# Modulation coefficients by sets of 128 features instead of 256, in a hybrid convolution and recurrence layer on one core

## Chip, core and metric

The kernel runs on one core of one Trainium2 chip. The metric is the device time in microseconds; the kernel before takes 1643.37 us (median of three runs, 1643.29 to 1644.09).

## What is computed

The layer has 256 latent tokens `x`, 256 context tokens `ctx` and 2048 features, all in float32. Only its first stage matters here. Both token streams are normalised, scaled and shifted, each with its own vectors (from `c` for the latents, from `c_ctx` for the context), and the result `h` goes into a large input projection:

```
mod = silu(c) @ w_mod + b_mod                   # w_mod 2048 x 12288, six vectors of 2048
sh_m, sc_m, ... = split(mod, 6)
h  = rms_norm(x,   norm_pre_mix) * (1 + sc_m)  + sh_m
hc = rms_norm(ctx, norm_pre_mix) * (1 + scc_m) + shc_m    # the same with silu(c_ctx)
p  = h @ w_in ;  pc = hc @ w_in[:, :3072]
```

The 4096 columns of `w_mod` that give `sh_m` and `sc_m` are 33.6 MB. They are read while the first products of `h` with `w_in` are made, because a block of 128 features of `h` needs only its own 128 scales and shifts.

## The kernel before

**Tiles and queue.** Weights come in tiles of 128 x 1024 floats (512 KB), all issued on SP's DMA queue in the order of a list (`Stream`, lines 414 to 427). A tile lands in one of 5 buffers called `raw`, or, if the list says `paged`, in one of 30 general pages of the same size (`page`, line 191; the trace calls it `rawpage`). `fetch_to(FETCH)` issues tiles ahead until 13 are held, 5 in `raw` buffers and 8 in pages (`RAWS`, `FETCH`, line 92). A page that is wanted while all 30 are held waits for the release of another. In this stage the pages also hold the inputs (8, until they are turned), the turned inputs `xT` (8, two blocks of 128 features each), the blocks `h` (one page each), and some single ones.

**Sets.** Features are handled in 8 sets of 256, that is two row blocks of 128 (loop at line 664). For one set the weights are 8 tiles. Of the 2048 rows of `w_mod`, the first 1536 (`KP` = 12 blocks of 128) go over TensorE: 12 products of a 128 x 32 operand `s32` (silu of both vectors, 2 of 32 columns used) with 128 x 512 weights (scale and shift of 256 features), four at a time in four column strips of 32 of the array (line 675). The last 512 rows go over VectorE: two tiles `wmd`, transposed on the host, and for each 4 multiplications with running sum (`sums`, line 648). `wmd` tiles lie in `raw` buffers, the other six in pages.

**From sums to h.** `modulate` (line 602) copies the TensorE sums to a row (ScalarE, line 605), turns it by 4 transposes, adds up the four strips (VectorE, line 612), adds the VectorE part and the bias, and has scale `A` and shift `B` of two blocks (lines 616, 619). Then, for each of the two blocks, ScalarE writes the rounded `h` and the full value back into `xT` (line 629, four instructions of 128 x 256), and VectorE writes the rest, their difference (line 632).

**Order on VectorE.** Calls of `issue_after` fix the order in which instructions are queued on an engine. `normed` (line 555, the multiplication of the next set's inputs by the reciprocal root mean square) is put behind the last line 632 of this set (line 703), and `sums` of the next set is put behind `normed` (line 665). So on VectorE one turn of the loop is: line 612, `A` and `B`, the two line 632, `normed`, the 8 sums of the next set, and line 612 again.

**Work between.** Tiles of `w_in` are split into a rounded part and a rest (`whi` on ScalarE, line 123, `wlo` on VectorE, line 126). `values` multiplies each block of `h` with half of a tile `wi0` (12 matmuls of 512 columns a block), `forget` with a quarter of a tile `wf0` (6 matmuls a block). They are generators whose pieces are put between the steps of `modulate` (lines 686 to 707), so that TensorE has work while the other engines make the next `h`. `values_begun` (24 matmuls) does blocks 0 and 1 of a second tile right after the first set. While the first set is awaited, TensorE makes 20 idle products in the same form (lines 676 to 678) and some `warm` matmuls. All TensorE instructions of the stage are queued in program order (`pe`, line 180).

Of the kernel before, what the change touches and what calls it, by code (L numbers as in the profile page):

```python
# [8 lines left out]
F32 = mybir.dt.float32  # L9
F32R = mybir.dt.float32r  # L10
# [27 lines left out]
KP = 12  # L38
FETCH = 13

# [11 lines left out]
class Stream:  # L52
# [76 lines left out]
    def next(self, ahead=AHEAD):  # L129
        while len(self.ready) < ahead and self.done < len(self.items):  # L130
            self.prepare()
        while ahead > 1 and self.done < len(self.items) and self.items[self.done][1] is not None:
            self.prepare()
        return self.ready.popleft()


class Kernel:
# [227 lines left out]
    def run(self):  # L365
# [143 lines left out]
        def block(k):  # L509

            return xT[k // 2][:, k % 2 * 512:(k % 2 + 1) * 512]
# [36 lines left out]

        def normed(c, *behind):

            x = xT[c][:, :TW].rearrange("p (j t) -> p j t", j=2)
            with ExitStack() as after:
                for ins in behind:
                    after.enter_context(self.tc.issue_after(ins.ins))
                self.last3 = nc.vector.tensor_tensor(x, x, rrow.rearrange("p (o t) -> p o t", o=1).broadcast_to([P, 2, 512]), op=ALU.mult)

# [15 lines left out]

        fq = collections.deque()

        def forget():
# [25 lines left out]

        def modulate(c, ps, part):

            row = self.small(512, "row")
            self.last = nc.scalar.copy(out=row, in_=ps)
            yield
            pt = self.bank()
            for j in range(4):
                self.pe(nc.tensor.transpose, out=pt[:, j * P:(j + 1) * P], in_=row[:, j * P:(j + 1) * P], identity=v["ident"])

            cols = self.small(8, "cols")
            nc.vector.tensor_reduce(cols.rearrange("p (j i) -> p j i", i=2), pt.rearrange("p (j g f) -> p j f g", j=4, g=4)[:, :, 0:2, :],
                                    axis=mybir.AxisListType.X, op=ALU.add)
            ks = slice(2 * c, 2 * c + 2)
            for n, dst in enumerate((Av, Bv)):
                nc.vector.tensor_tensor(dst[:, :, ks], cols[:, 4 * n:4 * n + 4].rearrange("p (b i) -> p i b", i=2),
                                        part[:, 4 * n:4 * n + 4].rearrange("p (b i) -> p i b", i=2), op=ALU.add)
                if n == 0:
                    self.scaled = nc.vector.scalar_tensor_tensor(dst[:, :, ks], dst[:, :, ks], 1.0,
                                                                 v["g_pm"][:, ks].rearrange("p (o k) -> p o k", o=1).broadcast_to([P, 2, 2]), op0=ALU.add, op1=ALU.mult)  # L620
            yield
            for k in range(2 * c, 2 * c + 2):
                hp.append(self.page(F32R, f"h{k}"))
                hi, lo = (hp[k].rearrange("p (i s t) -> p s i t", i=2, s=2)[:, n] for n in range(2))
                x = block(k).rearrange("p (i t) -> p i t", i=2)
                with self.tc.issue_after(self.his[-1].ins):
                    for o in (hi, x):
                        for i in range(2):
                            last = nc.scalar.activation(out=o[:, 1 - i], in_=x[:, 1 - i], func=AF.Identity, scale=Av[:, i, k:k + 1], bias=Bv[:, i, k:k + 1])  # L629
                for i in range(2):  # L630
                    hparts[i].append(hp[k][:, (1 - i) * 512:(2 - i) * 512])
                self.last2 = last, nc.vector.tensor_tensor(lo, x, hi.bitcast(F32), op=ALU.subtract)
                yield

        def sums(c, *behind):

            part = self.cp.tile([P, 8], F32, name="part", tag="part", bufs=2)
            for u in range(2):
                st.fetch_to(FETCH)
                w = st.whole()  # L640
                for b in range(2):
                    s = w[:, b * 512:(b + 1) * 512]
                    for i in range(2):
                        o = s if i else self.small(512, "junk")
                        with ExitStack() as after:
                            for ins in behind:
                                after.enter_context(self.tc.issue_after(ins.ins))
                            nc.vector.scalar_tensor_tensor(o, s, 1.0, srow[:, i * 512:(i + 1) * 512], op0=ALU.mult, op1=ALU.mult,
                                                           accum_out=part[:, 4 * u + 2 * b + i:4 * u + 2 * b + i + 1])
            for n in range(2):  # L650
                p = part[:, 4 * n:4 * n + 4].rearrange("p (b i) -> p b i", i=2)
                o = (1 - n) * KT + 2 * c
                nc.vector.tensor_tensor(p, p, v["bmod"][:, o:o + 2].rearrange("p (b o) -> p b o", o=1).broadcast_to([P, 2, 2]), op=ALU.add)
# [10 lines left out]
        for c in range(8):  # L664
            part = sums(c, self.last3)
            ps = self.bank()
            for t in range(KP // 2):
                st.fetch_to(FETCH)
                w = st.whole()
                for k2 in range(2):  # L670
                    k = 2 * t + k2
                    g = 32 * (k % 4)
                    self.pe(nc.tensor.matmul, ps[g:g + 32, :], s32[:, 32 * k:32 * k + 32], w[:, k2 * 512:(k2 + 1) * 512], start=(k < 4), stop=(k >= KP - 4))
                if c == 0 and t < KP // 2 - 1:

                    if t == 0:
                        idle = self.bank()
                    for g in range(0, P, 32):
                        self.pe(nc.tensor.matmul, idle[g:g + 32, :], s32[:, :32], srow[:, :512], start=True, stop=True)
            st.fetch_to(FETCH)  # L680

            mod = modulate(c, ps, part)
            next(mod)
            copied = self.last
            if c:
                next(forget)
            else:
                self.warm(5)
            next(mod)
            if c:  # L690
                next(forget)
            else:
                self.warm(8)
            parts(vq, copied, lo=[self.scaled])
            next(mod)
            if c == 0:
                parts(fq, *self.last2)
                parts(vq2, *self.last2)
            next(mod)
            if c % 2 and c < 7:  # L700
                parts(fq, *self.last2)
            if c < 7:
                normed(c + 1, *self.last2)
            for _ in range(2 if c else 1):
                next(values)
            for _ in range(2):
                next(forget)
            if c == 0:
                vb = self.values_begun(hx, vq2.popleft())
        for _ in values:  # L710
# [760 lines left out]
    def conv(self, uhv, uvv):  # L1471
# [73 lines left out]
_IN = [("pack", (P, NPACK), F32), ("x", (T, D), F32), ("ctx", (T, D), F32), ("bgain", (4, TW), F32), ("gain", (4, TW), F32), ("masks", (P, 7 * P), I32),  # L1545
       ("wm0", (4 * KP, P, TW), F32), ("wmd", (16, P, TW), F32), ("crow", (2, TW), F32), ("wmt", (64, P, TW), F32), ("wm1", (64, P, TW), F32), ("wi0", (16, P, TW), F32), ("wf0", (4, P, TW), F32), ("wi1", (80, P, TW), F32),
       ("wi2", (80, P, TW), F32),        ("wpw", (16, P, TW), F32), ("who", (16, P, TW), F32), ("wo", (32, P, TW), F32), ("w1", (128, P, TW), F32), ("w2", (128, P, TW), F32)]
# [76 lines left out]
```

## Time and profile before

| | |
|---|---|
| median of three runs | 1643.37 us |
| the profiled execution's own time | 1644.45 us |
| span of its instructions | 1642.7 us |
| TensorE busy | 1627.8 us, 99% of the span |
| VectorE busy | 1163.1 us, 71% |
| ScalarE busy | 799.9 us, 49% |
| bytes moved by DMA | 374.47 MB, 228 GB/s in the mean |

Times in the rows count from the span's start. PE is TensorE's matmuls, PEld its weight loads, DVE is VectorE, ACT is ScalarE, SP issues the DMAs. A float32 matmul that is not in the rounded format appears as two instructions, so the 12 products of a set are 24 rows. A matmul's length contains its latency: the next one can start long before it ends, so that paces are read from start to start.

### The profile page before, as it was taken

To read this page: it belongs to the slowest core of one execution; us is meant where nothing else is said; L and a number is where in the kernel's file an instruction comes from. 1 tells how busy PE (TensorE), PEld (TensorE's weight loads), DVE (VectorE), ACT (ScalarE), POOL (GpSimd) and SP (SyncE) were. 2 spreads that over 40 slices of the span, in tenths; PEclk is the share of its full clock that TensorE was granted. 3 is DMA by queue.
4 is the path that set the end of the run, shared out by engine and by line. 5 is a ranking of instruction groups with operands and counts; after the bars stand their busy time and mean duration, and the time that the engine had idled before them with its cause. 6 is when DMAs were issued, how large, how long until landed. Compare 5 with 4: busy or idle time off the path is not lost.

```text
span 1642.7 us, 22019 instructions
## 1 busy us (share of the span) xinstructions
PE 1627.8 (99%) x8211; PEld 1359.2 (83%) x8211; DVE 1163.1 (71%) x1703; ACT 799.9 (49%) x1142; POOL 8.1 (0%) x18
## 2 busy tenths in 40 slices
PE   8999999999999999999999999999999999999998
PEld 6668888888988888888888888888888888888887
DVE  7777777778868889967887766456655665566555
ACT  6553444443554444653446665445544554346543
POOL 0000000000000000000000000000000000000000
PEclk9999999999999999999999999999999999999999
DMA  9998954444656556688887376677667667666553
GB/s 375 389 395 292 318 163 149 154 142 141 204 185 227 189 187 210 228 277 294 317 291 269 136 233 204 212 237 240 219 205 232 233 214 215 232 219 195 190 192 116
DMA packets 103771, 374.47 MB, mean 228 GB/s; under 512 B 11632, under 2 KB 12400, under 8 KB 103664
## 3 DMA queue, kind: packets, MB, share of 16 engines
q1 hardware_dynamic: 102096, 368.60, 66.4%
q0 software_dynamic: 1280, 4.21, 0.9%
q8 instruction: 64, 1.05, 0.3%
q14 instruction: 43, 0.35, 0.1%
q10 hardware_dynamic: 288, 0.26, 0.0%
HBM read 370.93 MB, written 2.10 MB: 227 GB/s over the span
## 4 chain that ended last, share of the span: by engine, by line
PE 93%; DVE 2%; DMA 2%; ACT 1%; issue 1%; SPq 0%; ACTq 0%; DVEq 0%
PE bank L185 62%; PE bank L252 18%; PE bank L254 9%; PE bank L1396 2%; DMA raw<-wpw 1%; DVE wlo L126 1%; DMA x<-ctx 1%; DMA rawpage<-wm 1%; ACT whi L123 0%; PE bank L1427 0%; PE bank L1438 0%; PE bank L1436 0%; DVE gacc L1236 0%; SPq L498 0%; PE bank L1419 0%
## 5 line engine op out<-in xcount | busy, mean ns | idle before, releaser
L126 DVE TENSOR_TENSOR wlo<-raw,whi 128x1024 fp32r<-128x1024 f32 x488 | 594.7, 1224 | 356.2 <-ACT whi L123 348.4
L123 ACT ACTIVATE whi<-raw 128x1024 fp32r<-128x1024 f32 x488 | 513.4, 1059 | 577.7 <-PE bank L185 322.9
L185 PE MATMUL bank<-whi,h 128*128 128x512 f32 x1264 | 396.6, 392 | 0.8 <-ACT h L629 0.5
L252 PE MATMUL bank<-h,whi 128*128 128x512 f32 x1280 | 322.4, 394 | 0.0
L185 PEld LDWEIGHTS bank<-whi,h 128*128 128x128 f32 x1264 | 237.3, 188 | 50.9 <-DVE h L1085 0.7
L252 PEld LDWEIGHTS bank<-h,whi 128*128 128x128 f32 x1280 | 230.7, 189 | 41.3
L185 PE MATMUL bank<-wlo,h 128*128 128x512 f32 x632 | 246.9, 391 | 0.7 <-DVE wlo L126 0.5
L185 PE MATMUL bank<-whi,hidh 128*128 128x512 f32 x503 | 195.3, 388 | 0.0
L185 PE MATMUL bank<-wlo,hidh 128*128 128x512 f32 x503 | 195.3, 388 | 0.0
L185 PE MATMUL bank<-whi,hidl 128*128 128x512 f32 x503 | 195.3, 388 | 0.0
L254 PEld LDWEIGHTS bank<-h,wlo 128*128 128x128 f32 x1280 | 174.6, 190 | 12.6
L254 PE MATMUL bank<-h,wlo 128*128 128x256 f32 x1280 | 178.5, 283 | 0.0
L185 PE MATMUL bank<-h,whi 128*128 128x512 f32 x512 | 164.7, 403 | 0.0
L185 PEld LDWEIGHTS bank<-wlo,h 128*128 128x128 f32 x632 | 118.8, 188 | 26.5 <-DVE wlo L126 2.4
L185 PEld LDWEIGHTS bank<-whi,hidh 128*128 128x128 f32 x503 | 94.5, 188 | 19.3
L185 PEld LDWEIGHTS bank<-whi,hidl 128*128 128x128 f32 x503 | 94.5, 188 | 19.2
L185 PEld LDWEIGHTS bank<-wlo,hidh 128*128 128x128 f32 x503 | 94.5, 188 | 19.2
L185 PEld LDWEIGHTS bank<-h,whi 128*128 128x128 f32 x512 | 92.1, 189 | 21.4 <-issue 5.9
L185 PE MATMUL bank<-h,wlo 128*128 128x512 f32 x256 | 100.2, 391 | 0.0
L1236 DVE SCALAR_TENSOR_TENSOR gacc<-raw,silu_c,gacc 128x1024 f32<-128x1024 f32 x60 | 76.8, 1279 | 0.0
L1249 DVE SCALAR_TENSOR_TENSOR raw<-raw,silu_row 128x1024 f32<-128x1024 f32 x64 | 76.5, 1220 | 0.0
L185 PEld LDWEIGHTS bank<-h,wlo 128*128 128x128 f32 x256 | 48.1, 188 | 10.5 <-DVE wlo L126 0.3
(246 smaller groups left out, 1363.0 us busy)
## 6 DMA issues: line engine op xcount, KB each, us to landing
raw<-w SPq DMA_DIRECT2D x256, 512.0 KB, 4.3
raw<-wi SPq DMA_DIRECT2D x172, 512.0 KB, 4.4
raw<-wmt SPq DMA_DIRECT2D x64, 512.0 KB, 4.3
raw<-wm SPq DMA_DIRECT2D x64, 512.0 KB, 4.5
rawpage<-wm SPq DMA_DIRECT2D x48, 512.0 KB, 8.8
raw<-wo SPq DMA_DIRECT2D x32, 512.0 KB, 4.7
raw<-wmd SPq DMA_DIRECT2D x16, 512.0 KB, 8.6
raw<-who SPq DMA_DIRECT2D x16, 512.0 KB, 5.1
```

Of the source, the lines that this page charges most:

```text
L123: kn.his.append(nc.scalar.activation(out=hi, in_=raw, func=AF.Copy))
L126: kn.los.append(nc.vector.tensor_tensor(lo, raw, hi.bitcast(F32), op=ALU.subtract))
L185: ins = fn(*args, **kw)
L252: nc.tensor.matmul(bank, w[0][:, cut(i)], x(k)[2], start=(k == 0), stop=False)
L254: nc.tensor.matmul(bank[:, T:], w[1][:, cut(i)], x(k)[0], start=False, stop=(k == nk - 1))
L1236: nc.vector.scalar_tensor_tensor(acc, raw, s, acc, op0=ALU.mult, op1=ALU.add)
L1249: nc.vector.scalar_tensor_tensor(raw, raw, 1.0, self.srow, op0=ALU.mult, op1=ALU.mult, accum_out=self.dot[:, 32 * j + b:32 * j + b + 1])
L1396: nc.tensor.matmul(ps[:, b * P:(b + 1) * P], w, r, start=True, stop=True)
```

## The change

- Sets have 128 features, one block; there are 16. A set's matmuls have 256 columns (scale and shift of 128 features).
- In the first two sets all 16 row blocks go over TensorE (16 products, 4 tiles `wms`, no VectorE sums). In the other 14 a set has one tile `wmd` (4 sums) and three tiles `wm0` (12 products). The tiles of `w_mod` are 64 as before.
- All of them, `wmd` too, lie in pages; `FETCH` is 16, so up to 11 pages and 5 `raw` buffers are held ahead.
- In set k TensorE's queue has the products of the set, 3 matmuls of `forget`, 2 transposes, 3 matmuls of `forget`, 12 of `values`; from set 2 on all of these 18 are with block k-1. Blocks 0 and 1 of the second tile (24 matmuls) come in set 1. The idle products are 12, of 256 columns.
- The row's copy is queued behind ScalarE's last write for the block before, the reduction of line 612 behind the set's sums. Bias and scale are folded into two instructions for `A` and `B`.

```diff
-FETCH = 13
+WHOLE = 2
+FETCH = 16
...
-        for c in range(8):
-            for u in range(2):
-                st.add_whole(a["wmd"][2 * c + u])
-            for t in range(KP // 2):
-                st.add_whole(a["wm0"][KP // 2 * c + t], paged=True)
-            st.add(a["wi0"][c])
-            if c == 0 or c % 2 and c < 7:
-                st.add(a["wf0"][(c + 1) // 2])
-            if c == 0:
+        for k in range(KT):
+            if k < WHOLE:
+                for t in range(KT // 4):
+                    st.add_whole(a["wms"][KT // 4 * k + t], paged=True)
+            else:
+                st.add_whole(a["wmd"][k - WHOLE], paged=True)
+                for t in range(KP // 4):
+                    st.add_whole(a["wm0"][KP // 4 * (k - WHOLE) + t], paged=True)
+            if k % 2 == 0:
+                st.add(a["wi0"][k // 2])
+            if k == 0 or k % 4 == 3 and k < KT - 1:
+                st.add(a["wf0"][(k + 1) // 4])
+            if k == 1:
                 st.add(a["wi0"][8])
...
+        def modulate(k, ps, part):
+            row = self.small(T, "row")
+            with ExitStack() as after:
+                for ins in self.last2[:1] if k else ():
+                    after.enter_context(self.tc.issue_after(ins.ins))
+                self.last = nc.scalar.copy(out=row, in_=ps)
+            yield
+            pt = self.bank()
+            for j in range(2):
+                self.pe(nc.tensor.transpose, out=pt[:, j * P:(j + 1) * P], in_=row[:, j * P:(j + 1) * P], identity=v["ident"])
+            cols = self.small(4, "cols")
+            with ExitStack() as after:
+                if part is not None:
+                    after.enter_context(self.tc.issue_after(self.last5.ins))
+                nc.vector.tensor_reduce(...)
+            a_, b_ = cols[:, 0:2], cols[:, 2:4]
+            if part is not None:
+                nc.vector.tensor_tensor(a_, a_, part[:, 0:2], op=ALU.add)
+            self.scaled = nc.vector.tensor_scalar(out=Av[:, :, k], in0=a_, scalar1=bias1[:, k:k + 1], scalar2=v["g_pm"][:, k:k + 1], op0=ALU.add, op1=ALU.mult)
+            if part is not None:
+                self.scaled = nc.vector.scalar_tensor_tensor(Bv[:, :, k], b_, v["bmod"][:, k:k + 1], part[:, 2:4], op0=ALU.add, op1=ALU.add)
...
+            x = block(k).rearrange("p (i t) -> p i t", i=2)
+            with self.tc.issue_after(self.his[-1].ins):
+                for o in (hi, x):
+                    for i in range(2):
+                        last = nc.scalar.activation(out=o[:, 1 - i], in_=x[:, 1 - i], func=AF.Identity, scale=Av[:, i, k:k + 1], bias=Bv[:, i, k:k + 1])
...
+            self.last2 = last, nc.vector.tensor_tensor(lo, x, hi.bitcast(F32), op=ALU.subtract)
+            yield
+        def sums(k, *behind):
+            if k < WHOLE:
+                return None
...
+            for n in range(2):
+                s = w[:, n * 512:(n + 1) * 512]
                 for i in range(2):
+                    o = s if i else self.small(512, "junk")
...
+                        self.last5 = nc.vector.scalar_tensor_tensor(o, s, 1.0, srow[:, i * 512:(i + 1) * 512], op0=ALU.mult, op1=ALU.mult,
+                                                                    accum_out=part[:, 2 * n + i:2 * n + i + 1])
...
+        for k in range(KT):
+            part = sums(k, self.last3)
+            ps = self.bank()[:, :T]
+            nk = KT if k < WHOLE else KP
+            for t in range(nk // 4):
                 st.fetch_to(FETCH)
                 w = st.whole()
+                for j in range(4):
+                    g, n = 32 * j, 4 * t + j
+                    self.pe(nc.tensor.matmul, ps[g:g + 32, :], s32[:, 32 * n:32 * n + 32], w[:, j * T:(j + 1) * T], start=(t == 0), stop=(t == nk // 4 - 1))
...
+            mod = modulate(k, ps, part)
             next(mod)
             copied = self.last
+            if k:
                 next(forget)
...
             next(mod)
+            if k:
                 next(forget)
...
+            if k % 2 == 0:
+                parts(vq, copied, lo=[self.scaled])
+            if k == 1:
+                parts(vq2, copied, lo=[self.scaled])
             next(mod)
+            if k == 0 or k % 4 == 3 and k < KT - 1:
                 parts(fq, *self.last2)
+            if k < KT - 1:
+                normed(k + 1, *self.last2)
+            if k == 1:
+                vb = self.values_begun(hx, vq2.popleft())
+            else:
                 next(values)
```

`normed(k)` now multiplies one block (128 x 512), and `parts` splits a tile: `whi` on ScalarE behind the instructions named, `wlo` on VectorE.

## Rows read from the trace of the kernel before

**Rows 1.** The page's first part: engine, busy us (share of the span), instructions.

```profile
PE 1627.8 (99%) x8211; PEld 1359.2 (83%) x8211; DVE 1163.1 (71%) x1703; ACT 799.9 (49%) x1142; POOL 8.1 (0%) x18
```

**Rows 2.** The chain of waits that ended last, from 0 to 260 us, in order of time: start, length, what ran or was awaited.

```profile
5.35 11.43 DMA x<-ctx
...
31.40 37.88 PE bank L185 x199
...
70.73 8.92 DMA rawpage<-wm
...
79.69 24.57 PE bank L185 x128
...
104.30 64.03 PE bank L185 x294
```

**Rows 3.** The stretches of 10 us: start:end, length, then busy us (instructions) of PE, PEld, DVE, ACT and POOL, TensorE's granted clock as a share of full speed, DMA share, GB/s.

```profile
10.00:20.00 10.00, 9.89 (x74) 9.65 (x73) 8.41 (x15) 7.59 (x16) 0.00 (x0) 1.00 1.03 416
...
50.00:60.00 10.00, 10.00 (x57) 6.15 (x56) 9.56 (x26) 3.99 (x7) 0.00 (x0) 1.00 0.99 373
...
90.00:100.00 10.00, 10.00 (x58) 6.70 (x51) 7.35 (x24) 6.54 (x11) 0.00 (x0) 1.00 1.02 407
...
120.00:130.00 10.00, 10.00 (x46) 8.28 (x45) 4.16 (x5) 7.08 (x13) 0.00 (x0) 1.00 0.74 247
```

**Rows 4.** PE's instructions in order of time, from the inputs' last step to the first product with `h`: start, length, line, operation, count.

```profile
20.50 0.65 PE L185 MATMUL bank<-pack,r 128*128 128x128 f32 x4
21.08 0.62 PE L185 MATMUL bank<-rawpage,s 128*32 128x512 f32 x2
...
27.58 0.60 PE L185 MATMUL bank<-rawpage,s 128*32 128x512 f32 x2
28.11 0.77 PE L185 MATMUL bank<-ones_r 128*128 128x128 f32 x5
28.92 0.66 PE L185 MATMUL bank<-pack,row 128*128 128x128 f32 x4
...
30.89 0.50 PE L185 MATMUL bank<-whi,h 128*128 128x512 f32 x1 [0.47 <-ACT h L629]
31.40 0.50 PE L185 MATMUL bank<-wlo,h 128*128 128x512 f32 x1
```

**Rows 5.** PE's instructions in order of time around one set's products (the fourth set).

```profile
64.77 0.39 PE L185 MATMUL bank<-h,wlo 128*128 128x512 f32 x1
65.09 2.78 PE L185 MATMUL bank<-rawpage,s 128*32 128x512 f32 x24
67.80 0.73 PE L185 MATMUL bank<-h,whi 128*128 128x512 f32 x2
68.37 0.40 PE L185 MATMUL bank<-h,wlo 128*128 128x512 f32 x1
68.61 0.66 PE L185 MATMUL bank<-pack,row 128*128 128x128 f32 x4
69.02 0.71 PE L185 MATMUL bank<-h,whi 128*128 128x512 f32 x2
69.57 0.40 PE L185 MATMUL bank<-h,wlo 128*128 128x512 f32 x1
```

**Rows 6.** All engines in order of time in the middle of the second set's products; the count of a row takes in instructions that the window cuts off.

```profile
41.55 1.50 PE L185 MATMUL bank<-rawpage,s 128*32 128x512 f32 x12
...
42.01 0.13 PEld L185 LDWEIGHTS bank<-rawpage,s 128*32 128x32 f32 x4 [0.30 <-issue]
```

**Rows 7.** DVE's instructions in order of time, one turn of the loop (third set).

```profile
58.29 0.19 DVE L612 TENSOR_REDUCE cols<-bank 128x8 f32<-128x32 f32 x1
...
58.79 1.23 DVE L126 TENSOR_TENSOR wlo<-raw,whi 128x1024 fp32r<-128x1024 f32 x1
61.02 0.69 DVE L632 TENSOR_TENSOR h<-xT,h 128x512 fp32r<-128x512 f32 x1 [1.01 <-ACT xT L629]
63.00 0.69 DVE L632 TENSOR_TENSOR h<-xT,h 128x512 fp32r<-128x512 f32 x1 [1.28 <-ACT xT L629]
63.61 1.22 DVE L555 TENSOR_TENSOR xT<-xT,s 128x1024 f32<-128x1024 f32 x1
64.74 0.68 DVE L648 SCALAR_TENSOR_TENSOR junk<-raw,srow 128x512 f32<-128x512 f32 x1
...
69.71 0.19 DVE L612 TENSOR_REDUCE cols<-bank 128x8 f32<-128x32 f32 x1
```

**Rows 8.** ACT's instructions in order of time in the same set, its first block's four writes.

```profile
58.91 1.09 ACT L629 ACTIVATE h<-xT,B,A 128x256 fp32r<-128x256 f32 x2 [0.99 <-DVE A L619]
59.91 1.08 ACT L629 ACTIVATE xT<-xT,B,A 128x256 f32<-128x256 f32 x2
```

**Rows 9.** DVE's instructions in order of time after the second set's `h`, with a tile `wf0` split between.

```profile
52.18 1.22 DVE L126 TENSOR_TENSOR wlo<-raw,whi 128x1024 fp32r<-128x1024 f32 x1
53.32 0.69 DVE L648 SCALAR_TENSOR_TENSOR junk<-raw,srow 128x512 f32<-128x512 f32 x1
```

**Rows 10.** PE's instructions in order of time at the end of the stage, from the first product of the second `values` on.

```profile
130.09 0.39 PE L185 MATMUL bank<-whi,h 128*128 128x512 f32 x1
...
131.67 0.39 PE L185 MATMUL bank<-wlo,h 128*128 128x512 f32 x1
```

More of the change, by code (lines that the diff above doesn't have):

```diff
@@ L547, in turn_inputs, with normed @@
             nc.vector.tensor_copy(rrow, ps)
-        def normed(c, *behind):
-            x = xT[c][:, :TW].rearrange("p (j t) -> p j t", j=2)
+        def normed(k, *behind):
+            x = block(k)
             with ExitStack() as after:
@@ L554, in normed @@
                     after.enter_context(self.tc.issue_after(ins.ins))
[L555 removed]
+                self.last3 = nc.vector.tensor_tensor(x, x, rrow, op=ALU.mult)
         def hx(i):
@@ L573, in run @@
         fq = collections.deque()
+        bias1 = self.cp.tile([P, KT], F32, name="bias1")
+        nc.vector.tensor_scalar(out=bias1, in0=v["bmod"][:, KT:2 * KT], scalar1=1.0, scalar2=None, op0=ALU.add)
         def forget():
@@ L600, in run @@
         forget = forget()
-        def modulate(c, ps, part):
-            row = self.small(512, "row")
-            self.last = nc.scalar.copy(out=row, in_=ps)
+        def modulate(k, ps, part):
[4 more added lines that the diff above has]
+                self.last = nc.scalar.copy(out=row, in_=ps)
             yield
             pt = self.bank()
-            for j in range(4):
+            for j in range(2):
@@ L609, in modulate @@
                 self.pe(nc.tensor.transpose, out=pt[:, j * P:(j + 1) * P], in_=row[:, j * P:(j + 1) * P], identity=v["ident"])
[L611 to L620, printed above, removed]
@@ L621, in modulate @@
-            yield
[L622 to L629, printed above, removed]
-                for i in range(2):
-                    hparts[i].append(hp[k][:, (1 - i) * 512:(2 - i) * 512])
-                self.last2 = last, nc.vector.tensor_tensor(lo, x, hi.bitcast(F32), op=ALU.subtract)
-                yield
@@ L635, in sums @@
[L635 to L653, printed above, removed]
+            cols = self.small(4, "cols")
@@ new lines, in modulate @@
+            self.scaled = nc.vector.tensor_scalar(out=Av[:, :, k], in0=a_, scalar1=bias1[:, k:k + 1], scalar2=v["g_pm"][:, k:k + 1], op0=ALU.add, op1=ALU.mult)
+            if part is not None:
+                self.scaled = nc.vector.scalar_tensor_tensor(Bv[:, :, k], b_, v["bmod"][:, k:k + 1], part[:, 2:4], op0=ALU.add, op1=ALU.add)
+            else:
+                self.scaled = nc.vector.tensor_scalar(out=Bv[:, :, k], in0=b_, scalar1=v["bmod"][:, k:k + 1], scalar2=None, op0=ALU.add)
+            yield
@@ new lines, in modulate @@
+            hp.append(self.page(F32R, f"h{k}"))
+            hi, lo = (hp[k].rearrange("p (i s t) -> p s i t", i=2, s=2)[:, n] for n in range(2))
+            x = block(k).rearrange("p (i t) -> p i t", i=2)
[3 more added lines that the diff above has]
+                        last = nc.scalar.activation(out=o[:, 1 - i], in_=x[:, 1 - i], func=AF.Identity, scale=Av[:, i, k:k + 1], bias=Bv[:, i, k:k + 1])
+            for i in range(2):
+                hparts[i].append(hp[k][:, (1 - i) * 512:(2 - i) * 512])
@@ new lines, in modulate @@
+            self.last2 = last, nc.vector.tensor_tensor(lo, x, hi.bitcast(F32), op=ALU.subtract)
[3 more added lines that the diff above has]
+                return None
+            part = self.cp.tile([P, 4], F32, name="part", tag="part", bufs=2)
+            st.fetch_to(FETCH)
+            w = st.whole()
+            for n in range(2):
+                s = w[:, n * 512:(n + 1) * 512]
+                for i in range(2):
+                    o = s if i else self.small(512, "junk")
+                    with ExitStack() as after:
+                        for ins in behind:
+                            after.enter_context(self.tc.issue_after(ins.ins))
+                        self.last5 = nc.vector.scalar_tensor_tensor(o, s, 1.0, srow[:, i * 512:(i + 1) * 512], op0=ALU.mult, op1=ALU.mult,
+                                                                    accum_out=part[:, 2 * n + i:2 * n + i + 1])
@@ L663, in run @@
         normed(0)
[L664 to L667, printed above, removed]
+        for k in range(KT):
[3 more added lines that the diff above has]
+            for t in range(nk // 4):
                 st.fetch_to(FETCH)
                 w = st.whole()
[L670 to L674, printed above, removed]
+                for j in range(4):
+                    g, n = 32 * j, 4 * t + j
+                    self.pe(nc.tensor.matmul, ps[g:g + 32, :], s32[:, 32 * n:32 * n + 32], w[:, j * T:(j + 1) * T], start=(t == 0), stop=(t == nk // 4 - 1))
+                if k == 0 and t < nk // 4 - 1:
                     if t == 0:
@@ L678, in run @@
                     for g in range(0, P, 32):
-                        self.pe(nc.tensor.matmul, idle[g:g + 32, :], s32[:, :32], srow[:, :512], start=True, stop=True)
+                        self.pe(nc.tensor.matmul, idle[g:g + 32, :T], s32[:, :32], srow[:, :T], start=True, stop=True)
             st.fetch_to(FETCH)
-            mod = modulate(c, ps, part)
+            mod = modulate(k, ps, part)
             next(mod)
             copied = self.last
-            if c:
+            if k:
                 next(forget)
@@ L693, in run @@
                 self.warm(8)
-            parts(vq, copied, lo=[self.scaled])
+            if k % 2 == 0:
+                parts(vq, copied, lo=[self.scaled])
+            if k == 1:
+                parts(vq2, copied, lo=[self.scaled])
             next(mod)
-            if c == 0:
+            if k == 0 or k % 4 == 3 and k < KT - 1:
                 parts(fq, *self.last2)
[L698 to L704, printed above, removed]
+            if k < KT - 1:
+                normed(k + 1, *self.last2)
+            if k == 1:
+                vb = self.values_begun(hx, vq2.popleft())
+            else:
                 next(values)
[L706 to L709, printed above, removed]
         for _ in values:
@@ L1545 @@
 _IN = [("pack", (P, NPACK), F32), ("x", (T, D), F32), ("ctx", (T, D), F32), ("bgain", (4, TW), F32), ("gain", (4, TW), F32), ("masks", (P, 7 * P), I32),
-       ("wm0", (4 * KP, P, TW), F32), ("wmd", (16, P, TW), F32), ("crow", (2, TW), F32), ("wmt", (64, P, TW), F32), ("wm1", (64, P, TW), F32), ("wi0", (16, P, TW), F32), ("wf0", (4, P, TW), F32), ("wi1", (80, P, TW), F32),
+       ("wms", (WHOLE * KT // 4, P, TW), F32), ("wm0", ((KT - WHOLE) * KP // 4, P, TW), F32), ("wmd", (KT - WHOLE, P, TW), F32), ("crow", (2, TW), F32), ("wmt", (64, P, TW), F32), ("wm1", (64, P, TW), F32), ("wi0", (16, P, TW), F32), ("wf0", (4, P, TW), F32), ("wi1", (80, P, TW), F32),
        ("wi2", (80, P, TW), F32),        ("wpw", (16, P, TW), F32), ("who", (16, P, TW), F32), ("wo", (32, P, TW), F32), ("w1", (128, P, TW), F32), ("w2", (128, P, TW), F32)]
@@ L1583, in row, with by_block @@
         return w.reshape(8, 2, P, w.shape[1] // 512, 512).transpose(3, 0, 2, 1, 4).reshape(-1, P, TW)
+    def by_block(w):
+        n = w.shape[0] // P
+        return w.reshape(n // 4, 4, P, 2, KT, P)[:, :, :, ::-1].transpose(4, 0, 2, 1, 3, 5).reshape(-1, P, TW)
     parts = {
@@ L1599 @@
         "masks": _masks(),
-        "wm0": wm[:KP * P, :2 * D].reshape(KP // 2, 2, P, 2, 8, T)[:, :, :, ::-1].transpose(4, 0, 2, 1, 3, 5).reshape(-1, P, TW),
-        "wmd": wm[KP * P:, :2 * D].reshape(512, 2, 8, 2, P)[:, ::-1].transpose(2, 1, 4, 3, 0).reshape(-1, P, TW),
+        "wms": by_block(wm[:, :2 * D])[:WHOLE * KT // 4],
+        "wm0": by_block(wm[:KP * P, :2 * D])[WHOLE * KP // 4:],
+        "wmd": wm[KP * P:, :2 * D].reshape(512, 2, KT, P)[:, ::-1].transpose(2, 3, 1, 0).reshape(-1, P, TW)[WHOLE:],
         "crow": f(c).reshape(2, TW),
```

3 lines of the change are left out of this document (2 added, 1 removed).

## The prediction

> **What bounds the kernel now.** The page's first part comes first: TensorE is busy 99% of the span [rows 1]. From about 31 us on hardly any of its time is free, so whatever the change does to the end of the first stage, it does to the whole. The chain of waits says what holds TensorE back in that stage: the inputs' last DMA until 16.8, then TensorE alone, but for one wait for a `rawpage` tile at 79.65 [rows 2]. Between those two landings lie 48 tiles of the list (11, 10, 9 and 10 for the first four sets with their `wi0` and `wf0`, 8 for the fifth), so a tile lands every (79.65 - 16.78)/48 = 1.31 us. The stretches of 10 us show the DMA queue full, at 373 to 416 GB/s, to 120 us and not after [rows 3]. TensorE and DMA are thus nearly in balance, and the second set of rows to read is VectorE's: one turn of its loop, from one reduction (line 612) to the next, took 58.29 to 69.71, 11.42 us [rows 7], for two blocks of features. Such a turn cannot be hurried by other engines: reduction, `A` and `B`, ScalarE's writes, the rests, `normed`, the next sums, each behind the one before. The stage ends where the second `values` begins, at 130.09 [rows 10]; matmuls of 512 columns then start (131.67 - 130.09)/7 = 0.226 us apart (taken as 0.227).
>
> **The start: a gain.** The first set's products begin at 21.08, behind the inputs' last step, and end where the `warm` matmuls begin, at 28.11 [rows 4]. In these 7.03 us are 24 + 40 instructions, four at a time: 16 groups of 0.44 us. After the change there are 32 + 24, 14 groups, of half the columns. No row has a column strip with 256 columns. If the time follows the columns, a group takes 0.22, if nothing shrinks 0.44; I take 0.22, because the loads of the next group run while this one streams: a group's four loads end 0.13 us after they begin, and begin as the group starts [rows 6]. The products then end at 21.08 + 14 x 0.22 = 24.2; their four tiles are there at 16.8 + 4 x 1.31 = 22.0. From 28.11 to the second product with `h` (31.40; the first one waits for its partner's `wlo`) it is 3.29 us now, and two transposes fewer make 3.1. So the second product comes at 27.3 instead of 31.40: **4.1 us gained**.
>
> **Set 1.** Eleven more matmuls of block 0 end at 29.9. Set 1's products are 8 groups, 1.76, with 0.27 for going to strips and back: 65.00 to 65.09 on the way in, 2.71 - 6 x 0.44 = 0.07 on the way out, 0.11 more for the first pair [rows 5]. Their last tile, the tenth, lands at 29.9, in time. Then 6 matmuls of `forget` (1.36) and two transposes with their restart (0.41/2 + 0.1 = 0.30 [rows 5]) lead to 33.6. `values_begun` needs 24 x 0.227 = 5.45 and waits up to 1.2 us for the rest of its tile, since ScalarE's split waits for the row's copy and VectorE's for `A` and `B`; it ends at 40.3.
>
> **TensorE's own pace after that** is, for one block: 6 groups 1.32, switching 0.27, transposes 0.30, 18 matmuls 4.09, together 5.98 us. The products are no more than before, but switching and restarting are paid 16 times and not 8. The Trainium skill says in "TensorEngine Tiling (Array Packing)", Key Properties, that a change of the tiling mode drains the engine; the rows give 0.27 us to that and agree.
>
> **VectorE's turn: the loss.** With one block in a set the turn is [rows 7, 8]: reduction to ScalarE's first write 58.91 - 58.29 = 0.62, and 0.08 because `B` now follows `A`; four writes until the rest can start, 61.02 - 58.91 = 2.11; the rest 0.61; `normed` of 512 columns 0.61, as the rest, which has the same shape; four sums at (69.71 - 64.74 - 0.07)/8 = 0.61, 2.45. Sum 6.48 us for one block, where 11.42/2 = 5.71 was paid before. What is added is one more reduction chain and one more exposed rest for each pair. The split of an even set's `wi0` tile lies in the wait for ScalarE and costs nothing: now too `wlo` runs from 58.79, and VectorE then still waits 1.01 for ScalarE [rows 7]. A `wf0` tile's split does not fit there, because its ScalarE part comes behind the writes; it stands between `normed` and the sums and takes 53.32 - 52.18 = 1.14 [rows 9], after sets 3, 7 and 11. The waits that the change adds (row behind the writes, reduction behind the sums) are on this path already.
>
> How much of this does TensorE feel? `forget` of block k-1 needs its rest 0.70 + 2.11 + 0.69 = 3.5 us after the reduction, and TensorE comes to it 1.6 us after the start of set k. The reduction itself comes at the earliest 2.7 us after its set's start (1.32 products, 0.68 `forget`, transposes and copies), so there are 5.98 + 1.6 - 3.5 - 2.7 = 1.4 us in hand. VectorE loses 0.5 in each turn and 1.14 at every fourth; from set 4 on it sets the pace. Reduction of set 2: 40.3 + 2.7 = 43.0 (its sums are done before). Of set 15: 43.0 + 13 x 6.48 + 3 x 1.14 = 130.6. Then 3.5 to the rest of block 15, 4 + 6 matmuls that need it, 2.3: the stage ends at **136.4, 6.3 us later** than now. Behind it TensorE runs full, so that all of it stays.
>
> **DMA and pages.** Bytes are the same. The last `w_mod` tile is the 77th: 16.8 + 77 x 1.31 = 117.7, before set 15 on either pace (TensorE's comes to it at 40.3 + 13 x 5.98 = 118.0). `wmd` in pages frees `raw` buffers, and SP's queue has less to wait for. But the pages are short: at the start 18 + 11 + 2 (squares) are asked of 30, and at set 11 again 2 + 3 `xT` + 12 `h` + 2 + 11. Between nothing and one set's products (1.6) for each of sets 10 to 12, up to 5 us; I take nothing, because a slower loop leaves the queue ahead.
>
> **Sum.** -4.1 at the start, +10.4 in the loop: +6.3. The profiled span was 1642.7 us, its execution 1644.45, the median 1643.37; put on the median: **1649.7 us**. Terms off by 0.05 us in a turn make 0.7, the start another 1; its own range is 1646 to 1653.
>
> **Rivals.** (a) *TensorE's pace.* If VectorE's turn stays under 5.98 + its 1.4 in hand, the end is 40.3 + 14 x 5.98 + 18 x 0.227 = 128.1, 2.0 us earlier: **1641.4**. For it: finer sets hide each block's chain behind the products of the one before, and this kernel's waits for tiles (79.69 [rows 2]) go. Against: it needs a turn 0.5 us shorter and the `wf0` splits out of it, and every piece of the turn is a row. Without the wait in set 1 it comes to 1640. Chance 0.27. (b) *Strips do not shrink with the columns.* If a group's loads show after all, 0.13 for each, set 2 starts 2.8 later, TensorE needs 6.76 for a block, and the end is 43.1 + 14 x 6.76 + 4.1 = 141.8: **1655**; with groups of 0.44 still, 1665. Against it stand the loads [rows 6]. The Trainium skill's "TensorE: Matmul & The Clock Gate", Part 3, says that loads overlap running matmuls only where the row group differs, and here it is the same for all four strips; the trace speaks against that. Chance 0.06. (c) *Pages.* If `h` or tiles wait for pages, 5 us come on top: on TensorE's pace 1646.4, on VectorE's **1655**. Chance 0.07.
>
> **Numbers.** The forecast has 0.60. Some 0.2%, 3.3 us, is what a measurement of this kernel tells from no change, so faster means under 1640.1, slower over 1646.7. Faster: 0.12, of (a). Same: 0.06 of the forecast, 0.15 of (a), 0.04 of (c), 0.25. Slower: 0.54, 0.06 of (b), 0.03 of (c), 0.63. The range goes from rival (a) to (c): 1641 to 1655; below lies a part of (a), above most of (b).
>
> **What would show it.** Second product with `h` near 27.3; reductions of line 612 some 6.5 us apart from set 4 on, 7.6 where a `wf0` is split; VectorE idle only before line 632; TensorE with a wait of some 0.3 to 0.5 us in each set, put down to line 632; the second `values` at 136. Reductions 6.0 apart and TensorE without waits would be rival (a); 24 strip rows in over 2 us, (b); DMA or `h` waits in sets 10 to 12, (c).

## The result and the profile after

The changed kernel takes 1649.56 us (median of 6 runs, 1647.76 to 1650.92), the kernel before 1643.41 beside it (6 runs, 1643.29 to 1644.09). The ratio is 1.0034, interval 1.0025 to 1.0044: slower by about 6.1 us. The profiled execution of the changed kernel took 1650.6, its span is 1648.8 against 1642.7, and the granted clock is 0.999 of full speed in it.

The page, first and fourth part (the chain that ended last, shares of the span by engine and by line):

```profile
PE 1628.8 (99%) x8403; PEld 1362.2 (83%) x8403; DVE 1162.1 (70%) x1710; ACT 802.3 (49%) x1150; POOL 8.1 (0%) x18
...
PE 91%; DVE 5%; ACT 2%; issue 1%; DMA 1%; SPq 0%; ACTq 0%; DVEq 0%
```

TensorE's busy sum moved by 1.0 us only [rows 1], and by its share nothing has changed. The place of the loss is in the chain of waits, 0 to 260 us, longest pieces in order of time:

```profile
26.86 6.42 PE bank L186 x49
35.12 8.54 PE bank L186 x52
47.82 1.22 DVE junk L664 x4
49.04 1.23 DVE rawpage L664 x4
...
124.00 1.23 DVE rawpage L664 x4
128.76 46.56 PE bank L186 x205
```

Where the chain of before ran on TensorE [rows 2], it now runs from 43.7 to 128.8 on VectorE's sums (with ScalarE's writes, `normed` and the rest between). TensorE's next piece ends at 128.76 + 46.56 = 175.32, the same piece of before at 104.30 + 64.03 = 168.33 [rows 2]. So the stage itself costs **6.99 us**, of which 0.25 are inputs that landed later in this execution (the first strips start at 21.33, before at 21.08 [rows 4]).

TensorE in order of time, from the first strip product to the second set (start, length, line, what, count, wait):

```profile
21.33 0.64 PE L186 MATMUL bank<-rawpage,s 128*32 128x256 f32 x8
...
24.49 0.78 PE L186 MATMUL bank<-ones_r 128*128 128x128 f32 x5
...
26.86 0.50 PE L186 MATMUL bank<-whi,h 128*128 128x512 f32 x1 [0.51 <-ACT h L644]
27.35 0.50 PE L186 MATMUL bank<-wlo,h 128*128 128x512 f32 x1
...
30.21 1.93 PE L186 MATMUL bank<-rawpage,s 128*32 128x256 f32 x32
32.07 0.74 PE L186 MATMUL bank<-h,whi 128*128 128x512 f32 x2
...
33.80 0.40 PE L186 MATMUL bank<-whi,h 128*128 128x512 f32 x1
35.12 0.50 PE L186 MATMUL bank<-wlo,h 128*128 128x512 f32 x1 [0.92 <-DVE wlo L127]
...
41.03 1.50 PE L186 MATMUL bank<-rawpage,s 128*32 128x256 f32 x24
```

The first strips take 24.49 - 21.33 = 3.16 us where 7.03 were paid [rows 4], and the second product with `h` comes at 27.35 instead of 31.40. VectorE, one turn of its loop, from reduction (line 627) to reduction:

```profile
64.32 0.17 DVE L627 TENSOR_REDUCE cols<-bank 128x4 f32<-128x16 f32 x1
...
67.16 0.69 DVE L647 TENSOR_TENSOR h<-xT,h 128x512 fp32r<-128x512 f32 x1 [2.14 <-ACT xT L644]
67.77 0.68 DVE L560 TENSOR_TENSOR xT<-xT,s 128x512 f32<-128x512 f32 x1
68.37 0.68 DVE L664 SCALAR_TENSOR_TENSOR junk<-rawpage,srow 128x512 f32<-128x512 f32 x1
...
70.82 0.17 DVE L627 TENSOR_REDUCE cols<-bank 128x4 f32<-128x16 f32 x1
```

70.82 - 64.32 = 6.50 us for one block; two blocks had 11.42 [rows 7]. In this turn VectorE is idle only while ScalarE writes. That the reduction waits for VectorE's own sums and not for TensorE is seen at once in the view of the tile `cols`, 40 to 135 us (count, duration in ns, first and last start; then the idle time before it in us and how often):

```profile
L627 DVE TENSOR_REDUCE cols<-bank x14: 162/169/176, 43.7 to 131.7; 128x4 f32<-128x16 f32 x14
...
its engine sat idle before it (us, times) until:
  PE bank L186: 3.9, 1
```

Of 14 reductions only the first had VectorE waiting for TensorE. They lie 6.50 apart, or 7.64 after sets 3, 7 and 11, from 43.68 to 131.68. What TensorE feels stands in its rows of one set late in the stage:

```profile
120.03 1.50 PE L186 MATMUL bank<-rawpage,s 128*32 128x256 f32 x24
121.47 0.50 PE L186 MATMUL bank<-h,whi 128*128 128x512 f32 x1
122.23 0.49 PE L186 MATMUL bank<-h,whi 128*128 128x512 f32 x1 [0.27 <-DVE h L647]
...
126.53 1.50 PE L186 MATMUL bank<-rawpage,s 128*32 128x256 f32 x24
```

From set to set it is 126.53 - 120.03 = 6.50, VectorE's turn, and TensorE's wait is for the rest of `h` (line 647). Two more rows bear on DMA (stretches of 10 us, columns as in [rows 3]):

```profile
90.00:100.00 10.00, 9.75 (x69) 6.64 (x71) 7.56 (x25) 4.67 (x9) 0.00 (x0) 1.00 1.03 406
120.00:130.00 10.00, 9.43 (x76) 6.03 (x76) 8.48 (x21) 7.01 (x12) 0.00 (x0) 1.00 0.37 139
```

The queue still runs full at 90, at 120 it has fallen to 139 GB/s where before it was at 247 [rows 3], while the stage goes on: the last tile of `w_mod` landed at 118.89, ahead of its need (set 15 starts at 126.53). From 40 to 145 us TensorE waits for no tile, only for the rest of `h`. So DMA isn't the bound.

### The profile page after: what moved, and what is told of

The parts are those of the page before. It is cut to its first block, busy times and chain, and to the rows that moved or that the text cites. A ratio compares the mean times of both kernels' runs of the same rounds, so it can differ in the third digit from the quotient of the medians.

```text
span 1648.8 us, 22426 instructions
## 1 busy us (share of the span) xinstructions
PE 1628.8 (99%) x8403; PEld 1362.2 (83%) x8403; DVE 1162.1 (70%) x1710; ACT 802.3 (49%) x1150; POOL 8.1 (0%) x18
## 4 chain that ended last, share of the span: by engine, by line
PE 91%; DVE 5%; ACT 2%; issue 1%; DMA 1%; SPq 0%; ACTq 0%; DVEq 0%
PE bank L186 59%; PE bank L253 18%; PE bank L255 9%; PE bank L1405 2%; DVE rawpage L664 1%; DVE junk L664 1%; ACT h L644 1%; DVE wlo L127 1%; ACT xT L644 1%; DVE xT L560 0%; DMA x<-x 0%; DMA raw<-who 0%; PE bank L1436 0%; DVE h L647 0%; PE bank L1447 0%
```

## The experiments

The theory is that VectorE's serial turn of 6.5 us sets the pace, against 5.98 that TensorE needs. The rivals are TensorE's own 16 switches and strips, the pages, and DMA. Five kernels make one edit to the changed kernel, two add a second and a third edit to the first of these, and one edits the kernel before. The kernel before took 1643.91 and 1643.84 on the chips of the two series, and 1643.41 beside the changed kernel; differences from the changed kernel's 1649.56 carry these 0.5 us.

**Half of the sums out of the turn.** Two of the four sums are queued a set earlier, in VectorE's wait for ScalarE, and `wf0` moves up in the list, to the side of `wmd`.

```diff
+                if k % 4 == 0:
+                    st.add(a["wf0"][k // 4])
...
+            if WHOLE <= k + 1 < KT:
+                st.fetch_to(FETCH)
+                wd = st.whole()
+                part = self.cp.tile([P, 4], F32, name="part", tag="part", bufs=2)
+                sums(wd, part, 0, self.scaled)
             next(mod)
...
                 normed(k + 1, *self.last2)
+            if WHOLE <= k + 1 < KT:
+                sums(wd, part, 1, self.last3)
```

> Two of a set's four VectorE sums are queued one set earlier, behind A and B, where VectorE otherwise waits 2.1 us for ScalarE's four writes; the list has wmd of set k+1 before wf0. Theory (VectorE's turn of 6.5 us sets the pace): the turn falls to 6.48 - 1.22 = 5.3 us (6.4 where a wf0 is split), under TensorE's 5.98, so reductions stand 6.0 apart, TensorE's waits for line 647's rest (0.27 to 0.3 a set) go, and the stage ends at 41.0 + 14 x 5.98 + 4.1 = 128.9, 1.2 us before that of the kernel before: 1642.2 us, between 1641 and 1643.5. Rival (strips or pages make the loss): the order on VectorE changes nothing, 1648 to 1651.

It took 1644.4 us (1642.88 to 1646.08, 11 runs), 1.0004 of before [0.9996, 1.0013]: 5.2 less than the changed kernel, 2 more than expected. The turns were 5.96 in the mean to set 14, as expected, but the last took 9.3. All engines in order of time there:

```profile
117.63 1.06 ACT L124 ACTIVATE whi<-raw 128x1024 fp32r<-128x1024 f32 x1 [2.39 <-DMA raw<-wi]
...
121.44 0.50 PE L186 MATMUL bank<-h,whi 128*128 128x512 f32 x1 [1.21 <-DVE h L649]
121.45 1.06 ACT L124 ACTIVATE whi<-raw 128x1024 fp32r<-128x1024 f32 x1 [0.79 <-DMA raw<-wi]
122.41 0.35 ACT L619 COPY row<-bank 128x256 f32<-128x256 f32 x1
...
122.82 0.69 PE L186 MATMUL bank<-pack,row 128*128 128x128 f32 x2 [0.65 <-ACT row L619]
...
124.29 0.17 DVE L629 TENSOR_REDUCE cols<-bank 128x4 f32<-128x16 f32 x1
```

ScalarE waits 2.39 us for a tile of the second `values` (its split, line 124), which is queued ahead of block 14's writes; then again 0.79 ahead of the last row's copy. TensorE loses 1.21 + 0.65. Behind these two waits its granted clock falls to 0.50 of full speed, 1.2 GHz (columns as in [rows 3]):

```profile
123.00:126.00 3.00, 3.00 (x9) 2.42 (x9) 1.95 (x7) 0.98 (x2) 0.00 (x0) 0.50 0.43 120
```

The seven matmuls of 512 columns from 123.16 to 126.28 take 3.12 us, where seven at 0.227 take 1.59: another 1.5 in this execution. Three of the 11 runs have such a lower mean clock (0.998, the others 0.999), so that the median owes little to it. In the slower loop these tiles were there in time; the fast loop gets to them before the DMA queue does. So far this is read from the trace alone; the late splits below put it to the test.

**`normed` out of the turn.** The next block's multiplication goes ahead of the rest, and the sums follow it.

```diff
+            if k < KT - 1:
+                normed(k + 1, self.scaled)
             next(mod)
...
-            if k < KT - 1:
-                normed(k + 1, *self.last2)
```

> normed of set k+1 is queued behind A and B instead of behind the rest of block k; all four sums then follow it and stand before that rest. Theory: the turn is 4.4 us (odd sets) and 5.5 (even sets, with wlo), both under 5.98, but the rest of an even set comes 0.70 + 1.14 + 0.61 + 2.45 + 0.69 = 5.6 us after the reduction instead of 3.5. TensorE then waits for it (2.65 + 5.6 + 0.05) - (5.98 + 1.78) = 0.5 us in the seven even sets from 2 on and not in the odd ones: 3.7 us over the version with half of the sums ahead, 1645.9 us, between 1644.5 and 1647. If the turn alone counted, it would be 1642.2 as there; if VectorE's order did not matter, 1649.6.

It took 1645.02 (1644.23 to 1646.04, 11 runs), 1.0006 [0.9998, 1.0015], as expected. VectorE in one odd set:

```profile
77.67 0.68 DVE L664 SCALAR_TENSOR_TENSOR rawpage<-rawpage,srow 128x512 f32<-128x512 f32 x1
...
78.28 0.68 DVE L647 TENSOR_TENSOR h<-xT,h 128x512 fp32r<-128x512 f32 x1
...
80.61 0.18 DVE L627 TENSOR_REDUCE cols<-bank 128x4 f32<-128x16 f32 x1 [0.51 <-PE bank L186]
```

The rest follows the sums with no wait for ScalarE, and the reduction, though in this set a `wf0` split lies ahead of it, waits 0.51 for TensorE: the bound has changed sides. The turns alternate between 5.97 and 6.52, for in the even sets the `wi0` split no longer lies in a wait for ScalarE and makes the rest late, and TensorE waits for that.

**More work for TensorE.** Two matmuls of 128 columns, with no use, behind the transposes of each set from 2 on.

```diff
+            if k >= WHOLE:
+                for j in range(2):
+                    self.pe(nc.tensor.matmul, pt[:, T:T + P], self.ones_r, self.ones_r, start=True, stop=True)
```

> From set 2 on TensorE makes two more matmuls of 128 x 128 in each set, behind the transposes (0.23 us a set, 3.2 us in all); nothing reads them. Theory: TensorE waits 0.3 us in a set for VectorE, so that the filler disappears in the wait: 1649.6 us, at most 0.5 above the changed kernel. Rival (TensorE's own pace sets the stage): 3.2 us more, 1652.8.

It took 1649.81 (1649.36 to 1650.13, 5 runs), 1.0037 [1.0023, 1.005]: nothing. The waits of 40 to 145 us (total, times, longest), of TensorE for the rest; first the changed kernel, then with the added matmuls:

```profile
PE bank L186 <- DVE h L647: 5.1, 11, 1.2
```

```profile
PE bank L186 <- DVE h L650: 2.3, 2, 1.1
```

The added work took the place of a wait. The reductions run over 88.0 us in both. By the same reasoning the switching into strips and back is paid in time that TensorE has over; that alone was not taken away in a run.

**`wmd` in the `raw` buffers again**, with the number held ahead as before.

```diff
-FETCH = 16
+FETCH = 13
...
-                st.add_whole(a["wmd"][k - WHOLE], paged=True)
+                st.add_whole(a["wmd"][k - WHOLE])
```

> The changed kernel with wmd tiles in the five raw buffers and FETCH 13, as before the change. Theory: DMA is ahead of a loop that VectorE paces, so that where the tiles lie changes nothing: 1649.6 us within the spread of the changed kernel's runs (1647.8 to 1650.9). Rival (pages are what is short in the changed kernel, and squeeze h or tiles): up to 5 us less, 1645. If instead the raw buffers starve the queue as in the kernel before, more than 1651.

It took 1650.41 (1649.52 to 1651.62, 5 runs), 1.0041 [1.0029, 1.0054]: the pages that `wmd` takes cost nothing in this kernel, and bring nothing.

**One sum more** in each set, a product that is overwritten by the right one.

```diff
+                        if n + i == 0:
+                            nc.vector.scalar_tensor_tensor(o, s, 1.0, srow[:, 512:1024], op0=ALU.mult, op1=ALU.mult,
+                                                           accum_out=part[:, 0:1])
```

> The changed kernel with one VectorE sum more in each of the sets 2 to 15 (0.61 us; its result is overwritten by the next). Theory: every turn from set 3 on is 0.61 longer, 7.1 us instead of 6.5, and all of it is seen: 13 x 0.61 = 7.9 us more, 1657.5. Rival (VectorE is not what sets the pace): less than 2 us more.

It took 1658.94 (1657.22 to 1659.37, 4 runs), 1.009 [1.0077, 1.0104]: 9.4 more than the changed kernel, 1.5 more than expected. VectorE, two neighbouring reductions:

```profile
66.39 0.17 DVE L627 TENSOR_REDUCE cols<-bank 128x4 f32<-128x16 f32 x1
...
73.51 0.17 DVE L627 TENSOR_REDUCE cols<-bank 128x4 f32<-128x16 f32 x1
```

The turn is 7.12, that is 6.50 and one sum of 0.61, and all of it is felt. Only the last turn was 8.70: the stage is so late that three splits of the second `values` (3.49 us at 133.44) come between `A` and the rest, and ScalarE's part of the third stands ahead of that block's writes. These 1.6 are likely what is too much; no run took them away. The granted clock fell twice in this execution, too (0.50 from 93 to 95 and from 124 to 126 us), but the reductions around stayed 7.1 apart.

**Late splits.** To the first edit comes that the first three splits of the second `values` are queued behind block 15's rest.

```diff
         hlat = hx(0)
+        st.behind = [self.last2] * 3
         for _ in self.values(1, hx, st.next, vb):
```

> The version with half of the sums ahead, and the first three splits of the second values queued behind the last block's h on ScalarE. In the profile of that version ScalarE stood for 2.4 us before the split of such a tile, waiting for its DMA (landing 117.6), with the writes of block 14 queued behind it, and 0.8 us in set 15; the last two reductions were 9.3 us apart. Theory: with the queue free, all reductions from set 2 on are 6.0 apart, and the stage ends at 41.0 + 14 x 5.98 + 4.1 = 128.9: 3 us less than the version before, 1.2 us or more under the kernel before. Rival (the DMA itself is late by then, whatever ScalarE's queue): the wait moves to the set's products, no change against the version before.

It took 1642.01 (1640.75 to 1644.61, 11 runs), 0.9992 of before [0.9984, 1.0001]: 2.4 less than without, 1.8 less than before by the medians, though the interval takes in no change. So ScalarE's order was most of what the first edit fell short by; the granted clock is 1.00 from 120 to 130 us here. The tile `cols`, 40 to 125 us, and TensorE's strips in two neighbouring sets:

```profile
L629 DVE TENSOR_REDUCE cols<-bank x14: 169/174/177, 41.7 to 119.2; 128x4 f32<-128x16 f32 x14
...
its engine sat idle before it (us, times) until:
  PE bank L186: 6.6, 8
```

```profile
62.92 1.50 PE L186 MATMUL bank<-rawpage,s 128*32 128x256 f32 x24
...
68.88 1.50 PE L186 MATMUL bank<-rawpage,s 128*32 128x256 f32 x24
```

The 14 reductions lie in 77.5 us, 5.96 each in the mean (5.63 to 6.56), and 8 of them wait for TensorE, whose sets start 5.95 to 6.00 apart from set 2 on: this is TensorE's own pace, without a wait in the turn. (This profile's inputs came some 2 us earlier than in the changed kernel's, first strips at 19.12 against 21.33, so its absolute times are early by that.)

**An early split in set 1.** The split of `wi0[8]` goes ahead of the row's copy, against TensorE's wait of 0.92 at 35.12.

```diff
+            if k == 1:
+                parts(vq2)
             mod = modulate(k, ps, part)
...
-            if k == 1:
-                parts(vq2, copied, lo=[self.scaled])
```

> As the last, and in set 1 the tile wi0[8] is split before the row's copy instead of behind it and behind A and B. Theory: values_begun no longer waits 0.9 us for the rest of that tile, set 2 starts 0.9 us sooner, and all of it stays: 0.9 us less than the version without it, 2 to 3 us under the kernel before. Rival (the DMA bounds the finer sets): the 0.9 us come back as waits for tiles, no change.

It took 1642.4 (1641.68 to 1643.34, 11 runs), 0.9992 [0.9983, 1.0]: nothing gained. TensorE in set 1:

```profile
36.22 0.73 PE L186 MATMUL bank<-whi,h 128*128 128x512 f32 x2 [1.19 <-DVE h L649]
```

The wait went from the tile's rest to the next thing due, the rest of block 1. Neither DMA nor the split set that time; block 1's chain did.

**The same in the kernel before.** In sets 2 to 7, four of its eight sums are queued a set earlier.

```diff
+            if 0 < c < 7:
+                st.fetch_to(FETCH)
+                wd = st.whole()
+                ahead = self.cp.tile([P, 8], F32, name="part", tag="part", bufs=2)
+                half(wd, ahead, 0, 0, self.scaled)
             next(mod)
+            if 0 < c < 7:
+                half(wd, ahead, 0, 1, *self.last2)
```

> The kernel before, with four of the eight VectorE sums of sets 2 to 7 queued one set earlier, in VectorE's waits for ScalarE's writes. Theory: there VectorE's turn (11.4 us, 12.6 with a wf0) only follows a TensorE that needs 11.6 and waits for tiles; a shorter turn gives nothing, within 1 us of the kernel before. Rival (the kernel before is paced by VectorE as well, and finer sets are no worse than large ones): 3 us or more faster.

It took 1642.25 (1641.47 to 1643.97, 11 runs), 0.9989 [0.998, 0.9998]: 1.6 us faster, a little outside of what was expected. The waits of SP's queue, 0 to 140 us, before and with this edit:

```profile
SPq L85 <- DVE raw L648: 24.1, 5, 5.7
SPq L85 <- DVE wlo L126: 23.7, 11, 4.5
```

```profile
SPq L85 <- DVE raw L645: 18.1, 8, 4.4
...
SPq L85 <- DVE wlo L126: 13.4, 10, 3.5
```

TensorE in before didn't wait for VectorE, but the queue did: a `raw` buffer comes free when its sums or its split are done. With earlier sums the queue waits less for VectorE, and a gap of 2.77 us between two landings at 42.3 is gone. That this is all of the 1.6 us wasn't tried. The finer sets with their sums ahead and late splits took 1642.01 in the same series: with the sums moved in both, 11 runs of each show no difference between the two sizes of sets.

## Why the prediction was right

The forecast was 1649.7, and 1649.56 was measured. Step by step:

- **The start.** Second product with `h` at 27.35, forecast 27.3. The 14 groups took 3.16, 0.226 each, forecast 0.22. The step that was open (do strips shrink with their columns) is settled by the rows: in set 1 eight groups run from 30.21 to 32.07, 0.23 each. With the loads showing, as rival (b) had it, it would have been 0.22 + 0.13 = 0.35 each, 2.8. The Trainium skill says in "TensorE: Matmul & The Clock Gate", Part 3, that loads overlap running matmuls only where the row group differs; the trace disagrees, for the four strips share theirs.
- **Set 1.** The wait was forecast at up to 1.2; from 33.80 to 35.12 TensorE lost 1.32 - 0.23 = 1.09. Set 2 began at 41.03, forecast 40.3. That 0.7 was the largest miss up to there: 0.2 had come up by 33.80 (forecast 33.6), and the 24 matmuls with their wait took 41.03 - 33.80 = 7.23, forecast 5.45 + 1.2 = 6.65, by short waits between them. The inputs landed 0.25 later than in the profile of before, but from the strips' end to the second product it was 27.35 - 24.49 = 2.86, forecast 3.1, which made up for that.
- **TensorE's own pace.** 5.98 was forecast. The changed kernel shows it while the 1.4 us in hand last: its sets 2 to 5 start at 41.03, 46.99, 52.98 and 58.93, the next only at 65.73. VectorE was forecast to set the pace from set 4 on; TensorE first waits for it in set 5. The version with late splits shows 5.96 throughout.
- **VectorE's turn.** 6.48 and 7.62 forecast, 6.50 and 7.64 measured. Each piece is where it was put: 67.16 - 64.32 = 2.84 to the rest (0.62 + 0.08 + 2.11 = 2.81), 0.61 the rest, 0.60 `normed`, 2.45 the four sums.
- **How much TensorE feels.** The reduction of set 15 came at 131.68, forecast 130.6: 0.7 of that is set 2's lateness, 0.3 are 13 turns of 0.02. TensorE's later work is 6.99 us behind, forecast 6.3.
- **The stage's end.** The last step did not go as forecast. All engines in order of time, behind the last reduction:

```profile
131.76 1.21 DVE L127 TENSOR_TENSOR wlo<-raw,whi 128x1024 fp32r<-128x1024 f32 x1
...
133.21 0.39 PE L186 MATMUL bank<-wlo,h 128*128 128x512 f32 x1
...
133.41 1.09 ACT L644 ACTIVATE h<-xT,B,A 128x256 fp32r<-128x256 f32 x2 [4.25 <-DVE A L632]
...
135.52 0.69 DVE L647 TENSOR_TENSOR h<-xT,h 128x512 fp32r<-128x512 f32 x1 [2.15 <-ACT xT L644]
```

  A split of the second `values` came between the reduction and `A`, so that the rest of block 15 followed its reduction by 135.52 - 131.68 = 3.84 us, forecast 2.81. By the forecast's path (the rest's end and 2.3 of matmuls) the stage would have ended at 135.52 + 0.69 + 2.3 = 138.5, 8.4 late. TensorE didn't wait: block 14's twelve matmuls begin at 130.25, the one at 133.21 is the fourteenth, and block 15's `h` is first written at 133.41, so it was in the second `values` by then, which is not bound to the stage's program order. The sign "second `values` at 136" thus failed, and that 6.99 lies near 6.3 is in this step luck.
- **Back again.** That the whole comes out at 6.1 and not 7.0 wasn't foreseen. TensorE's last group of four starts at 1642.96 against 1636.43, 6.53 behind, and the span ends 6.1 behind. Of the first 0.46 a possible source is a `wlo` that TensorE waits for at 798.55 in the kernel before, 0.54 us, where the changed kernel waits 0.3 in the same stretch; this stays open, and so does the 0.4 in the last steps. The agreement to 0.15 us is thus partly the meeting of a miss of +0.7 and one of -0.9.
- **DMA and pages.** Taken as nothing; the run with `raw` buffers measured nothing (0.85 us between medians, within the spread of 3 us that runs of the changed kernel show).

The rivals: (a) was not what happened, but its price was near. It had 1641.4 for TensorE's pace, if the turn were 0.5 us shorter and without the `wf0` split; the version with half of the sums ahead and late splits, whose turn no longer holds TensorE, gave 1642.0. (b) fell to the strips' rows, (c) to the run with `raw` buffers and, on TensorE's pace, to the version with late splits, where from 40 to 145 us TensorE waits for no tile. That switching makes the changed kernel's loss, which the added matmuls tested, fell too; at TensorE's own pace it is paid.

So the change was lost on VectorE's side: the turn holds one exposed reduction chain and one exposed rest for each block, where there had been one chain for two blocks. On TensorE's side it won little. From the first strips to the next stage's first matmul it is 168.17 - 21.08 = 147.09 us before, 175.16 - 21.33 = 153.83 in the changed kernel, and 165.15 - 19.12 = 146.03 with late splits: VectorE's turn and ScalarE's order cost 7.8, and of the 4.3 that the start gains by this count TensorE's own pace, with its wait in set 1 and its switching for each block, leaves 1.1.

## What to carry to other kernels

When a loop step is halved, list what is paid once for each step on the engine with the serial chain, not only the work that is divided: here 0.79 us more for each block on VectorE (6.50 for 5.71) made a 70% busy engine the bound of a 99% busy one. Whether it has become the bound is read from one view: before which instruction of the turn that engine is idle, and for whom. Work that depends on nothing in the turn (sums, inputs' scaling) belongs into the engine's wait inside the turn; and when the loop gets faster, look at what other queues hold for later stages, since a transfer that was in time no longer is. Try the new order on the old step as well: here it gave the kernel before 1.6 us, about as much as the finer sets have with it.

## What the runs showed of the hardware

- A group of four column strips takes 0.43 to 0.44 us at 512 columns and 0.22 to 0.23 at 256 (two instructions a product in float32): their loads, which took 0.13 us for four in [rows 6], stay hidden even at 256 columns.
- The inputs' landing differs from one execution to the next: the step on TensorE that follows the inputs' last statistics starts at 18.54 in one profile of these kernels and at 20.94 in another, and all later times of the stage move with it. Two kernels' traces are therefore compared by distances inside a stage, and differences of 1 us need many runs.
- TensorE's granted clock was 1.00 in every stretch of 10 us of this stage (from 10 us on) but those of two runs. With half of the sums ahead it was 0.50 (1.2 GHz) from 123 to 126 us, behind waits of 1.21 and 0.65 us; with one sum more it was 0.50 from 93 to 95 and from 124 to 126, each time behind waits of 0.70 and 1.21 us, while the same two waits before 136.29 and 138.01 brought no fall. Matmuls of 512 columns then start 0.43 us apart instead of 0.227. With one sum more the reductions stayed 7.1 apart through both falls, so that the loop lost nothing by them; with half of the sums ahead seven matmuls took 1.5 us more.
